# The perceptron of a two-layer decoder trunk takes x before its norm's row factor, and the planner that orders the kernel's instructions gets other costs

## The chip, the cores and the metric

One core of a Trainium2 chip runs the whole program. The metric is the device time of one execution in microseconds (us); lower is better. The shape is one sequence of 256 tokens, 1024 channels, two layers, float32.

## The reference, cut to what matters

Each layer has a mixing part (three branches whose merged result goes through `w_out`) and a perceptron with squared ReLU. Both are normed before and after:

```python
def rmsnorm(x, g):
    y = x * lax.rsqrt(jnp.mean(x * x, axis=-1, keepdims=True) + EPS)
    return y * g

for l in range(DEPTH):
    ...
    x = x + rmsnorm(merged @ w_out[l], ln_mix_post[l])
    h = rmsnorm(x, ln_mlp_pre[l])
    x = x + rmsnorm(jnp.square(jax.nn.relu(h @ mlp_w1[l])) @ mlp_w2[l], ln_mlp_post[l])
```

The norm multiplies each row of x by one positive number c (its row factor) and each column by a gain. As c is positive, relu(c·h) squared is c² times relu(h) squared, so c may be left out ahead of `mlp_w1` and c² be put on the result of `mlp_w2`.

## The kernel before

**Numbers and tiles.** Tokens are two tiles of 128 rows (t = 0, 1). Every float32 product runs as three products of parts: ScalarE copies an operand into a rounded part `hi`, VectorE subtracts it from the original into `lo`, and TensorE adds hi·hi, hi·lo and lo·hi in one PSUM bank. Weights come as units of 256 rows by 512 columns through SP's queue into five buffers (`raw`) and are split by ScalarE (`whi`) and VectorE (`wlo`) into four. Activations that stand as the contracted operand are needed transposed: four 128x128 transposes into a bank (`tr`), then the copy and the subtraction into `hmh` and `hml` (an object `XT`).

**The order of the work is planned while the program is built.** Side work is written as generators ("lanes") that yield the engine they want next ("A" ScalarE, "D" VectorE, "G" GpSimd, "P1" TensorE with one free bank). `Order` keeps a modelled clock for every engine, `Meter` (its call is line 140, so nearly all instructions of the trace carry that line) adds a modelled cost for each instruction, and after each weight row block (6 matmuls of 512 columns, or 12 of 256) `side` emits what the model says is ready by TensorE's modelled clock. `drain` forces a lane to its end where the next matmul needs it. Each engine then runs its instructions in the order in which they were emitted. The model's cost of a matmul of n columns is, in us,

```python
load = args[1].shape[1] / 1200.0
cost = max(load, 0.0025 + n / 2400.0) * (4 if args[1].dtype == F32 else 1)
```

and the modelled clock of the arrival of data is `dma_clock`.

**The jobs** follow each other in a written list per layer (`ORDER0`, `ORDER1`). Layer 0 starts `xr1 xr0 yr0 yr1 vm0 km0`: four projections of the normed x, then the keys and values of the memory tokens. The memory's norm is a lane that `mem_prep(0)` spawns during the first job, `start`, with a first due time of `dma_clock + 2.0`. It begins with a sum of squares of each loaded half tile of `mem` on ScalarE (`half_sumsq`, result tile `junk`); its transposes are needed at `vm0`.

**The boundary between mixing and perceptron.** `wo` multiplies by `w_out` into four banks, one for each token tile and half of the columns. When a bank is done, `Residual.half` sums its squares (ScalarE, `junk`) and multiplies it by the post-norm's gain (VectorE, `yg`). When both halves of a token tile are done, `finish` works out the row factor on GpSimd (`mean`, `var`, `rstd`) and adds the result to x (`xt`, VectorE). Then the next norm follows on the same engines in `norm_lane` and `half_lane`: sums of squares of the new x (`junk`), `mean`, `var`, `rstd`, the scaled row `hn` = x · factor · gain (VectorE), four transposes, two copies of 256 columns, two subtractions of 256 columns. `u0`, the first 512 columns of `mlp_w1`, needs them. In layer 0 the list puts `+vm0 +km0` (memory keys and values of layer 1) between `wo` and `u0`. In layer 1 nothing stands between, but there `wo` and `u0` run token tile 0 first and then token tile 1 (`skew`, `up_by_token`), so that one tile's boundary can run beside the other's matmuls; and `wo`'s weights can be split ahead of time into spare buffers (`we`). At the other boundary, after `d7`, the same `Residual` is used, followed by the next layer's norm, or in layer 1 by the store of the output.

Of the kernel before, what the change touches and what calls it, by code (L numbers as in the profile page):

```python
# [11 lines left out]
F32 = mybir.dt.float32  # L12
# [3 lines left out]
AF = mybir.ActivationFunctionType  # L16
# [89 lines left out]
class Meter:  # L106
# [5 lines left out]
    def __getattr__(self, name):  # L112
        fn, key, order = getattr(self.eng, name), self.key, self.order

        def call(*args, **kw):
            out = kw["out"] if "out" in kw else args[0]
            n = elems(out)
            if key == "A":
                cost = 0.055 + n / 1200.0
                cost += 0.06 * sum(not isinstance(kw.get(k, 0.0), float) for k in ("scale", "bias"))  # L120
                cost += 0.12 if kw.get("accum_out") is not None else 0.0
                if args[2] in TABLES:
                    cost += 1.28 * (self.table != TABLES[args[2]])
                    self.table = TABLES[args[2]]
            elif key == "D":
                if "reduce" in name:
                    n = elems(args[1])
                cost = DCOST + n / (1920.0 if name == "tensor_scalar" else 960.0)
                cost += 0.06 * (name == "scalar_tensor_tensor")
            elif key == "P":  # L130
                if name == "transpose":
                    cost = 0.109
                else:
                    load = args[1].shape[1] / 1200.0
                    cost = max(load, 0.0025 + n / 2400.0) * (4 if args[1].dtype == F32 else 1)
            else:
                cost = 0.25
            aps = [v.tensor.name for v in (*args, *kw.values()) if hasattr(v, "tensor")]
            order.note(key, cost, out.tensor.name, aps if "out" in kw else aps[1:])
            return fn(*args, **kw)  # L140

        return call
# [3 lines left out]
def trunk_kernel(ctx, tc, x, mem, positions, ln_mix_pre, w_in, conv_w, conv_b, lru_wr, lru_br, lru_wi, lru_bi,  # L146
# [48 lines left out]
    def f(ap):  # L195
        return ap.bitcast(F32)
# [191 lines left out]
            res.append(gt)  # L388
        return res

    def half_sumsq(src):

        j = a([P, 512], BF16, "junk")
        s = tiny([P, 1], name="ss")
        act.activation(j, src, AF.Square, scale=1.0 / 32, accum_out=s)
        return s

    def eps_lane(s, box):
        yield "G"
        m = tiny([P, 1], name="mean")  # L400
        pool.tensor_scalar(m, s, EPS, None, op0=OP.add)
        box.append(m)

    def first_half(src):

        box = []
        return spawn(eps_lane(half_sumsq(src), box), prio=0), box

    def rstd_of(m0, s1):
        v = tiny([P, 1], name="var")  # L410
# [108 lines left out]
    def normed(name):  # L519

        return lambda u, t: [f"{name}{v}{u // 2}" for v in range(NT) if t in (v, None)]

    class Residual:


        def __init__(self, t, tag, gt, g2, o, name):
            self.t, self.tag, self.gt, self.g2, self.o, self.name = t, tag, gt, g2, o, name
            self.g, self.ss = {}, {}

        def half(self, h, acc):  # L530
            def sums():
                yield "A"
                if h == 0:
                    el, self.box = first_half(acc)
                    yield el
                else:
                    self.s1 = half_sumsq(acc)

            def gain():
                yield "D"  # L540
                self.g[h] = a([P, 512], F32, "yg")
                dve.tensor_tensor(self.g[h], acc, self.gt[h], op=OP.mult)

            def both():
                yield [self.ss[h], gl]
                free(self.tag)

            self.ss[h] = spawn(sums(), prio=0)
            gl = spawn(gain(), prio=0)
            self.ss[h, "g"] = gl  # L550
            spawn(both(), prio=0)
            if h:
                spawn(self.finish(), prio=0)

        def finish(self):
            t = self.t
            yield [self.ss[0], self.ss[1]]
            yield "G"
            r = rstd_of(self.box[0], self.s1)
            ss = [None, None]  # L560

            def add(h):
                yield self.ss[h, "g"]
                yield "D"
                dve.scalar_tensor_tensor(xt[t][h], self.g[h], r, xt[t][h], op0=OP.mult, op1=OP.add)
                if self.o is None:
                    nc.sync.dma_start(out=out[0, t * P:(t + 1) * P, 512 * h:512 * h + 512], in_=xt[t][h])
                    return
                yield "A"
                if h == 0:  # L570
                    el, ss[0] = first_half(xt[t][0])
                    yield el
                else:
                    ss[1] = half_sumsq(xt[t][1])

            yield [spawn(add(h), prio=0) for h in range(2)]
            if self.o is not None:
                yield from norm_lane(xt[t], t, self.g2, self.o, self.name, ss)


# [763 lines left out]
    def layer(l):  # L1344
# [258 lines left out]
        def wo_done(t, hf, o):  # L1603
            if t == 0 and hf == 0:
                E["XM"] = XT("hm")
                E["res"] = [Residual(t, "at", *E["g_mix"], E["XM"], f"bnd{l}a") for t in range(NT)]
            E["res"][t].half(hf, o)
            if t == 1 and hf == 1:
                E["g_mlp_post"] = gain_tile(ln_mlp_post[l:l + 1, :])

        def wo_job():

            st = {}
            units = [Unit(w_out[l], 256 * k, 512 * hf) for k in range(4) for hf in range(2)]

            def begin():
                E["g_mix"] = gain_tile(ln_mix_post[l:l + 1, :]), gain_tile(ln_mlp_pre[l:l + 1, :])
                st["b"] = [[bank([P, 512], "at", "wo") for _ in range(2)] for _ in range(NT)]

            def mm(ui, u, i, only):  # L1620
                k, hf = 2 * (ui // 2) + i, ui % 2
                for t in range(NT) if only is None else (only,):
                    xh, xl = (v(k, t * P, (t + 1) * P) for v in (E["mg"].h, E["mg"].l))
                    o = st["b"][t][hf]
                    pe.matmul(o, xh, u.hi[i], start=(k == 0), stop=False)
                    pe.matmul(o, xh, u.lo[i], start=False, stop=False)
                    pe.matmul(o, xl, u.hi[i], start=False, stop=(k == KC - 1))
                    if k == KC - 1:
                        wo_done(t, hf, o)

            return Job(units, begin, mm, unit_need=lambda u, t: [f"mg{l}{u // 4}{v}" for v in range(NT) if t in (v, None)],
                       steps=[(u, t) for t in range(NT) for u in range(8)] if l == 1 else None, early=l == 1)
# [27 lines left out]
        def down_job(b):  # L1660
            units = [Unit(mlp_w2[l], 512 * b + 256 * kk, 512 * hf) for hf in range(2) for kk in range(2)]

            def begin():
                if b == 0:
                    E["acc"] = [[bank([P, 512], "at", "acc") for _ in range(2)] for _ in range(NT)]
                if b == 7:
                    g2 = o = None
                    if l + 1 < DEPTH:
                        g2, o = E["g_next"], XT("hT")
                        env[l + 1]["X"] = o  # L1670
                    E["res"] = [Residual(t, "at", E["g_mlp_post"], g2, o, f"bnd{l}b") for t in range(NT)]

            def mm(ui, u, i, only):
                hf, kk = ui // 2, ui % 2
# [66 lines left out]
        for b in range(8):  # L1741
            J[f"u{b}"], J[f"d{b}"] = up_job(b), down_job(b)

    def const_lane():
        yield "P1"
        pt = bank([P, P], "at", "pet")
        pe.transpose(pt, per.rearrange("p u d -> p (u d)"), ident)
        yield "D"
        dve.tensor_copy(pet, pt)
        free()  # L1750
        yield from rope_tables()

    def mem_prep(l):
        ms = []
        gm = gain_tile(ln_mem[l:l + 1, :])
        for t in range(NT):
            ms.append([])
            for h in range(2):
                m = a([P, 512], F32, "mem")
                nc.sync.dma_start(out=m, in_=mem[0, t * P:(t + 1) * P, 512 * h:512 * h + 512])  # L1760
                ms[t].append(m)
        env[l]["M"] = XT("mT")
        dma_clock[0] = max(dma_clock[0], od.T["D"] - 4.0) + 6 * 0.73
        od.cur.r = max(od.cur.r, dma_clock[0] + 2.0)
        spawn(norm_both(ms, gm, env[l]["M"], f"mnorm{l}"))

    def load_x(t):
# [28 lines left out]
    def start():  # L1796
        first_pre()
        mem_prep(0)
        prows = load_params()
        load_consts()  # L1800
        od.cur.r = 26.0
        spawn(prm_lane(prows), "prm")
        od.cur.r = 36.0
        spawn(const_lane(), "const")
# [35 lines left out]
```

## Time and profile before

| | us |
|---|---|
| median of 3 runs | 1221.04 |
| lowest and highest run | 1216.6, 1221.95 |
| the profiled execution's own time | 1221.59 |
| its span, first to last instruction | 1219.9 |

The mean granted TensorE clock over the span is 0.995 of full speed. PE is TensorE, ACT ScalarE, DVE VectorE, POOL GpSimd, SP the queue that issues DMAs. Matmuls are pipelined and their ends are modelled: a matmul that is listed with 283 ns can be followed by the next after 120 ns, so "busy" doesn't show small gaps.

### The profile page before, as it was taken

Reading aid. Unit: us, or ns where it says so; the run is one execution under the profiler, and the core shown is the slowest. Engines: PE = TensorE matmul, PEld = TensorE weight load, DVE = VectorE, ACT = ScalarE, POOL = GpSimd, SP = SyncE. Lnnn points to the kernel's source line nnn. Section 1 sums busy time; section 2 is a strip of 40 time slices with the busy share of each in tenths; the row PEclk is TensorE's granted clock in tenths of the full one; section 3 lists DMA queues with packets and bytes.
Section 4 is the critical chain, followed back from the end, with each engine's and each line's share of the span. In section 5 each row is a group of like instructions: output and inputs, shape, how many; then the busy total and the mean of one; then the engine's idle time right before and its main releaser. Section 6 shows DMA issues by size and latency. Waiting matters only on the chain.

```text
span 1219.9 us, 19570 instructions
## 1 busy us (share of the span) xinstructions
PE 1199.6 (98%) x7371; PEld 1068.8 (88%) x7371; DVE 901.6 (74%) x1516; ACT 736.7 (60%) x1330; POOL 35.5 (3%) x88
## 2 busy tenths in 40 slices
PE   8899999999999999999999999999999999999997
PEld 7899988888888889998989999888888887899896
DVE  4778897979898686555557587998978877655555
ACT  4677856777666465445456688675656655645443
POOL 3000000000000020000001000000000001000000
PEclk9899999999999999999999999999999999999999
DMA  8555656753345666666656556584534356565561
GB/s 283 181 161 168 190 156 181 223 152 108 122 131 186 233 191 191 194 189 189 206 174 210 154 171 176 153 258 140 154 121 138 121 164 217 166 187 183 190 190 69
DMA packets 121263, 212.58 MB, mean 174 GB/s; under 512 B 10441, under 2 KB 24098, under 8 KB 121169
## 3 DMA queue, kind: packets, MB, share of 16 engines
q1 hardware_dynamic: 120752, 211.19, 55.9%
q8 instruction: 58, 0.95, 0.3%
q0 software_dynamic: 416, 0.15, 0.1%
q14 instruction: 37, 0.30, 0.1%
HBM read 208.16 MB, written 1.05 MB: 172 GB/s over the span
## 4 chain that ended last, share of the span: by engine, by line
PE 92%; DVE 2%; DMA 2%; ACT 2%; issue 1%; SPq 0%; POOL 0%; POOLq 0%; DVEq 0%; ACTq 0%
PE mm L140 62%; PE acc L140 14%; PE ob L140 2%; PE sc L140 2%; PE wo L140 2%; PE pt L140 2%; PE hid L140 1%; PE gp L140 1%; PE mo L140 1%; PE msc L140 1%; PE tr L140 1%; DMA mem<-in_mem_dram 1%; ACT junk L140 1%; DVE wlo L140 1%; DMA raw<-in_mlp_w_dram 1%
## 5 line engine op out<-in xcount | busy, mean ns | idle before, releaser
L140 DVE TENSOR_TENSOR wlo<-raw,whi 128x1024 fp32r<-128x1024 f32 (+1 forms) x371 | 447.1, 1214 | 225.7 <-ACT whi L140 224.3
L140 ACT ACTIVATE whi<-raw 128x1024 fp32r<-128x1024 f32 (+1 forms) x371 | 385.3, 1055 | 204.9 <-PE mm L140 117.0
L140 PE MATMUL mm<-hmh,whi 128*128 128x256 f32 x480 | 135.9, 283 | 0.0
L140 PE MATMUL mm<-hmh,wlo 128*128 128x256 f32 x480 | 135.9, 283 | 0.0
L140 PE MATMUL mm<-hml,whi 128*128 128x256 f32 x480 | 135.9, 283 | 0.0
L140 PE MATMUL mm<-hTh,whi 128*128 128x256 f32 x448 | 129.4, 289 | 0.0
L140 PE MATMUL mm<-whi,hTh 128*128 128x512 f32 x320 | 129.1, 403 | 0.0
L140 PE MATMUL mm<-hTh,wlo 128*128 128x256 f32 x448 | 127.6, 285 | 0.0
L140 PE MATMUL mm<-hTl,whi 128*128 128x256 f32 x448 | 127.6, 285 | 0.0
L140 PE MATMUL mm<-wlo,hTh 128*128 128x512 f32 x320 | 125.1, 391 | 0.0
L140 PE MATMUL mm<-whi,hTl 128*128 128x512 f32 x320 | 125.0, 391 | 0.0
L140 PE MATMUL acc<-whi,rh 128*128 128x512 f32 x256 | 99.8, 390 | 0.0
L140 PE MATMUL acc<-wlo,rh 128*128 128x512 f32 x256 | 99.8, 390 | 0.0
L140 PE MATMUL acc<-whi,rl 128*128 128x512 f32 x256 | 99.6, 389 | 0.0
L140 PEld LDWEIGHTS mm<-hmh,whi 128*128 128x128 f32 x480 | 92.1, 192 | 0.5
L140 PEld LDWEIGHTS mm<-hml,whi 128*128 128x128 f32 x480 | 92.1, 192 | 0.5
L140 PEld LDWEIGHTS mm<-hmh,wlo 128*128 128x128 f32 x480 | 92.1, 192 | 0.0
L140 PEld LDWEIGHTS mm<-hTh,whi 128*128 128x128 f32 x448 | 86.9, 194 | 0.2
L140 PEld LDWEIGHTS mm<-hTl,whi 128*128 128x128 f32 x448 | 86.9, 194 | 0.2
L140 PEld LDWEIGHTS mm<-hTh,wlo 128*128 128x128 f32 x448 | 86.7, 194 | 0.0
L140 PEld LDWEIGHTS mm<-whi,hTl 128*128 128x128 f32 x320 | 60.1, 188 | 13.1
L140 PEld LDWEIGHTS mm<-whi,hTh 128*128 128x128 f32 x320 | 60.2, 188 | 12.0 <-issue 0.2
(311 smaller groups left out, 2467.7 us busy)
## 6 DMA issues: line engine op xcount, KB each, us to landing
raw<-in_w_in_dram SPq DMA_DIRECT2D x136, 512.0 KB, 3.7
raw<-in_mlp_w_dram SPq DMA_DIRECT2D x128, 512.0 KB, 4.2
raw<-in_w_mem_kv_dram SPq DMA_DIRECT2D x32, 512.0 KB, 4.2
raw<-in_cmp_w_dram SPq DMA_DIRECT2D x16, 512.0 KB, 4.0
raw<-in_w_br_rnn_dram SPq DMA_DIRECT2D x16, 512.0 KB, 3.7
raw<-in_w_br_mem_dram SPq DMA_DIRECT2D x16, 512.0 KB, 3.7
raw<-in_w_br_nsa_dram SPq DMA_DIRECT2D x16, 512.0 KB, 3.7
raw<-in_w_out_dram SPq DMA_DIRECT2D x16, 512.0 KB, 4.5
```

The source lines that it names most:

```text
L140: return fn(*args, **kw)
```

## The change

In five places:

1. `raw_lane` replaces `norm_lane` after `wo`: x itself is transposed, and the copy and the subtraction apply the pre-norm's gain as one number per partition (`col(k)`, from `mcol`, eight columns per layer). They are now made for 128 columns at a time, in turn: copy, subtraction, copy, subtraction, four pairs for each half. The row factor is made beside it in `factor_lane`, at lower priority.
2. The `Residual` behind `mlp_w2` takes that factor: its sums of squares read their scale from a tile, and the multiplication by the gain becomes one with the factor and the gain.
3. `mcol` needs one more small DMA on GpSimd's queue behind the ten that are there, one transpose and one copy at a planned 40 us. The broadcast gain tile of `ln_mlp_pre` (two DMAs of 256 KB per layer) goes.
4. The planner's cost of a matmul: 0.0133 in place of 0.0025 us beside the columns; for float32 operands 0.001.
5. The memory norm of layer 0 is due 12 us after `dma_clock` in place of 2 us. Layer 1 keeps 2 us.

```diff
-                    cost = max(load, 0.0025 + n / 2400.0) * (4 if args[1].dtype == F32 else 1)
+                    cost = (max(load, 0.0133 + n / 2400.0) if args[1].dtype != F32 else 4 * max(load, 0.001 + n / 2400.0))
...
+    def raw_lane(src, col, t, h, o):
+
+        yield "P1"
+        pt = bank([P, 4, P], "at", "tr")
+        for i in range(4):
+            pe.transpose(pt[:, i, :], src[:, i * P:(i + 1) * P], ident)
+        tq = slice(t * P, (t + 1) * P)
+        for i in range(4):
+            k = 4 * h + i
+            yield "A"
+            act.activation(o.h(k, t * P, (t + 1) * P), pt[:, i, :], AF.Copy, scale=col(k))
+            yield "D"
+            dve.scalar_tensor_tensor(o.l(k, t * P, (t + 1) * P), pt[:, i, :], col(k), f(o.h(k, t * P, (t + 1) * P)),
+                                     op0=OP.mult, op1=OP.subtract)
+        free()
+
+    def factor_lane(t, res):
+
+        yield "A"
+        el, box = first_half(xt[t][0])
+        s1 = half_sumsq(xt[t][1])
+        yield el
+        yield "G"
+        v = tiny([P, 1], name="var")
+        pool.tensor_tensor(v, box[0], s1, op=OP.add)
+        yield "D"
+        dve.reciprocal(res[:, 0:1], v)
+        dve.tensor_scalar(res[:, 1:2], res[:, 0:1], 1.0 / 32, None, op0=OP.mult)
...
-                dve.tensor_tensor(self.g[h], acc, self.gt[h], op=OP.mult)
+                if self.factor is None:
+                    dve.tensor_tensor(self.g[h], acc, self.gt[h], op=OP.mult)
+                else:
+                    dve.scalar_tensor_tensor(self.g[h], acc, self.factor[:, 0:1], self.gt[h], op0=OP.mult, op1=OP.mult)
...
+                if self.col is not None:
+                    yield spawn(raw_lane(xt[t][h], self.col, t, h, self.o), f"{self.name}{t}{h}", prio=0)
+                    return
...
-            if self.o is not None:
+            if self.col is not None:
+                yield spawn(factor_lane(t, self.res), f"{self.name}f{t}", prio=1)
+            elif self.o is not None:
                 yield from norm_lane(xt[t], t, self.g2, self.o, self.name, ss)
...
-                E["g_mix"] = gain_tile(ln_mix_post[l:l + 1, :]), gain_tile(ln_mlp_pre[l:l + 1, :])
+                E["g_mix"] = gain_tile(ln_mix_post[l:l + 1, :])
...
-                    E["res"] = [Residual(t, "at", E["g_mlp_post"], g2, o, f"bnd{l}b") for t in range(NT)]
+                    for t in range(NT):
+                        drain(f"bnd{l}af{t}")
+                    E["res"] = [Residual(t, "at", E["g_mlp_post"], g2, o, f"bnd{l}b", factor=E["r2"][t]) for t in range(NT)]
...
-        od.cur.r = max(od.cur.r, dma_clock[0] + 2.0)
+        od.cur.r = max(od.cur.r, dma_clock[0] + (2.0 if l else 12.0))
...
+        row = a([8 * DEPTH, P], F32, "mrow")
+        nc.gpsimd.dma_start(out=row, in_=ln_mlp_pre.rearrange("l (k c) -> (l k) c", c=P))
+        od.cur.r = 40.0
+        spawn(mcol_lane(row), "mcol")
```

## Rows read from the trace of the kernel before

**Rows 1.** Page: busy us, share of the span and instructions of each engine.
```profile
PE 1199.6 (98%) x7371; PEld 1068.8 (88%) x7371; DVE 901.6 (74%) x1516; ACT 736.7 (60%) x1330; POOL 35.5 (3%) x88
```

**Rows 2.** Windows by stage: length, busy us of five engines, PE clock, DMA share, GB/s.
```profile
0.00:50.00 50.00, 41.02 (x291) 40.27 (x292) 27.65 (x64) 27.14 (x52) 13.22 (x40) 0.90 0.74 238
...
210.00:410.00 200.00, 199.91 (x1101) 168.31 (x1100) 171.72 (x345) 136.47 (x316) 1.89 (x6) 1.00 0.51 158
410.00:446.00 36.00, 36.00 (x171) 29.97 (x170) 25.46 (x32) 19.01 (x35) 7.27 (x12) 1.00 0.66 217
...
780.00:1006.00 226.00, 224.61 (x1228) 188.53 (x1227) 196.08 (x392) 141.08 (x314) 0.00 (x0) 1.00 0.51 155
...
1026.00:1040.00 14.00, 11.20 (x57) 8.65 (x56) 7.70 (x15) 7.56 (x23) 3.49 (x9) 1.00 0.18 62
```

**Rows 3.** Waits of PE: what waited for what, us in total, times, longest.
```profile
PE tr L140 <- DVE hn L140: 9.2, 5, 3.2
...
PE gn L140 <- DVE wlo L140: 0.9, 1, 0.9
```

**Rows 4.** Timeline of ACT, 0 to 56 us: start, us, instructions, [idle before, releaser].
```profile
20.11 1.06 ACT L140 ACTIVATE whi<-raw 128x1024 fp32r<-128x1024 f32 x1 [0.74 <-PE mm L140]
28.34 0.63 ACT L140 ACTIVATE junk<-mem 128x512 bf16<-128x512 f32 x1 [7.17 <-DMA mem<-in_mem_dram]
...
31.95 2.00 ACT L140 ACTIVATE whi<-raw 128x1024 fp32r<-128x1024 f32 x2
```

**Rows 5.** Windows around the first stall of PE, columns as in Rows 2.
```profile
34.97:40.78 5.81, 5.81 (x27) 5.81 (x28) 5.60 (x14) 2.36 (x6) 0.00 (x0) 0.50 0.91 266
31.65:42.17 10.52, 7.36 (x42) 7.20 (x41) 8.72 (x23) 4.81 (x10) 0.42 (x1) 0.68 0.59 168
```

**Rows 6.** Instructions on tile raw, 22.7 to 22.8 us: the next weight unit behind mem.
```profile
L341 SPq DMA_DIRECT2D raw<-in_w_in_dram x1: 613/613/613, 22.8 to 22.8; - x1
DMA to landing us min/median/max: 8.9/8.9/8.9
```

**Rows 7.** Chain that ended last, whole span, in order of time: start, us, what.
```profile
42.42 8.63 PE mm L140 x72
...
250.48 1.59 PE mm L140 x6
254.88 1.38 PE mm L140 x6
...
1079.60 10.91 PE acc L140 x48
```

**Rows 8.** The same chain at layer 1's boundary, 1000 to 1062 us.
```profile
1024.72 0.76 DVE xt L140
...
1027.90 0.76 DVE hn L140
...
1028.71 0.67 PE tr L140 x4
...
1029.40 0.67 ACT hmh L140 x2
...
1030.09 0.04 DVE hml L140
...
1031.51 0.64 DVE yg L140
...
1032.17 0.70 ACT junk L140 x2
```

**Rows 9.** ACT's groups with shapes kept apart: busy us, mean ns, idle before.
```profile
L140 ACT ACTIVATE hTh<-tr,gcol 128x256 fp32r<-128x256 f32 x8 | 3.2, 479 | 2.7 <-PE tr L140 2.7
...
L140 ACT ACTIVATE hid<-hidT 128x128 f32<-128x128 f32 x6 | 1.4, 276 | 4.9 <-PE hidT L140 4.9
```

**Rows 10.** DVE's groups with shapes kept apart, columns as in Rows 9.
```profile
L140 DVE SCALAR_TENSOR_TENSOR hTl<-tr,gcol,hTh 128x256 fp32r<-128x256 f32 x8 | 3.3, 476 | 1.3 <-ACT hTh L140 1.3
...
L140 DVE TENSOR_TENSOR vx<-mm,vx 128x128 fp32r<-128x128 f32 x16 | 3.8, 278 | 0.0
```

More of the change, by code (lines that the diff above doesn't have):

```diff
@@ L389, in gain_tile, with half_sumsq @@
         return res
-    def half_sumsq(src):
+    def half_sumsq(src, scale=1.0 / 32):
         j = a([P, 512], BF16, "junk")
         s = tiny([P, 1], name="ss")
-        act.activation(j, src, AF.Square, scale=1.0 / 32, accum_out=s)
+        act.activation(j, src, AF.Square, scale=scale, accum_out=s)
         return s
@@ L402, in eps_lane, with first_half @@
         box.append(m)
-    def first_half(src):
+    def first_half(src, scale=1.0 / 32):
         box = []
-        return spawn(eps_lane(half_sumsq(src), box), prio=0), box
+        return spawn(eps_lane(half_sumsq(src, scale), box), prio=0), box
     def rstd_of(m0, s1):
@@ L521, in normed, with __init__ @@
         return lambda u, t: [f"{name}{v}{u // 2}" for v in range(NT) if t in (v, None)]
+    def raw_lane(src, col, t, h, o):
[23 more added lines that the diff above has]
+        dve.tensor_scalar(res[:, 1:2], res[:, 0:1], 1.0 / 32, None, op0=OP.mult)
     class Residual:
-        def __init__(self, t, tag, gt, g2, o, name):
+        def __init__(self, t, tag, gt, g2, o, name, factor=None, col=None, res=None):
             self.t, self.tag, self.gt, self.g2, self.o, self.name = t, tag, gt, g2, o, name
+            self.factor, self.col, self.res = factor, col, res
+            self.scale = 1.0 / 32 if factor is None else factor[:, 1:2]
             self.g, self.ss = {}, {}
@@ L533, in sums @@
                 if h == 0:
-                    el, self.box = first_half(acc)
+                    el, self.box = first_half(acc, self.scale)
                     yield el
                 else:
-                    self.s1 = half_sumsq(acc)
+                    self.s1 = half_sumsq(acc, self.scale)
             def gain():
@@ L1605, in wo_done @@
                 E["XM"] = XT("hm")
-                E["res"] = [Residual(t, "at", *E["g_mix"], E["XM"], f"bnd{l}a") for t in range(NT)]
+                E["r2"] = [sp.tile([P, 2], F32, tag="r2", bufs=2 * NT, name=nm("r2")) for _ in range(NT)]
+                col = lambda k: mcol[:, 8 * l + k:8 * l + k + 1]
+                E["res"] = [Residual(t, "at", E["g_mix"], None, E["XM"], f"bnd{l}a", col=col, res=E["r2"][t])
+                            for t in range(NT)]
             E["res"][t].half(hf, o)
@@ L1742, in layer, with mcol_lane @@
             J[f"u{b}"], J[f"d{b}"] = up_job(b), down_job(b)
+    mcol = cp.tile([P, 8 * DEPTH], F32, name="mcol")
+    def mcol_lane(row):
+        yield "P1"
+        pt = bank([P, 8 * DEPTH], "at", "mcol")
+        pe.transpose(pt, row, ident[:8 * DEPTH, :8 * DEPTH])
+        yield "D"
+        dve.tensor_copy(mcol, pt)
+        free()
     def const_lane():
```

## The prediction

> **What bounds the kernel now.** I read the page first. TensorE is busy for 1199.6 of 1219.9 us, VectorE 74%, ScalarE 60% [rows 1]: time can only come from where PE waits, or runs slowly. [...] So I counted waits and rates, in this order.
>
> The windows by stage show where PE is not busy: 9.0 us of the first 50, 0.1 of the 200 us from 210, nothing at layer 0's boundary (410 to 446), 1.4 from 780 to 1006, 2.8 of the 14 us at layer 1's boundary (1026 to 1040) [rows 2]. The list of PE's waits puts 9.2 us, five waits, on transposes `tr` that wait for `hn`, the scaled rows of a norm; the longest is 3.2 us. Next comes one wait of 0.9 us for `wlo` [rows 3]. Two places hold nearly all that the change can win.
>
> The first is at 31.7 us. ScalarE ends a weight copy at 21.2 us, and the next thing in its queue is the first sum of squares of `mem`, whose data land at 28.3: 7.2 us idle. The weight unit that PE needs next is copied only at 31.95, behind the four sums [rows 4]. [...] The second is layer 1's boundary: in the chain `xt` (1024.72) is followed by sums, factor and `hn` (1027.90), and only then by `tr` (1028.71) [rows 8].
>
> **The change part by part. The memory norm due 10 us later.** ScalarE was free for its sums at 21.2, so their due time lay no later than about there; 10 us on is 31.2 us or more, and the data land at 28.3 [rows 4], 2.9 us before. The weight copies then go first. Their data: the unit queued behind `mem` was issued at 22.75 and landed 8.9 us later [rows 6], at 31.7. A copy takes 1.0 us (2.00 for two [rows 4]), and I take the subtraction of the same width a little longer, at 1.2, so the unit stands at about 34, while PE, with the units split before it, needs it at 31.7 + 24 · 0.120 = 34.5 (0.120 us is 8.63/72 [rows 7]). A thin margin, but one.
>
> What is won: between 31.65 and 42.17 PE did 24 matmuls of 256 columns and 16 transposes (the count of 42 has two that began before) [rows 5]. At the full rate the matmuls are 2.9 us, and the transposes, of 128 columns, at no more than the same 0.120, 1.9: together 4.8. They took 10.5: 5.7 us to win, of which some 3.2 are the wait and the rest clock. What is late next is the transposes again, 10 us later in PE's order. ScalarE now reaches the sums only behind two weight copies that can't begin before 31.7, at about 34, and the chain from sums to transposes is 3.2 us (from the end of `xt`'s first half, 1024.72 + 0.76, to 1028.71 [rows 8]): 37.2. In the plan the sums stood between the weight copy that ended at 21.2 and the result of the first job some 4 us later, so their new place is 31.2 to 35, the middle 33.2, and by the model's own costs (two sums of 0.6, two GpSimd steps of 0.25, 0.66 for `hn`, the changes of engine) the transposes follow 3.0 to 3.2 later, at 36.4. PE would wait about 0.8 us; side work enters only after 12 matmuls, a grid of 1.4 us, so 0 to 2.2. I take 5.7 − 0.8 = **4.9 us won**, bounds 3.5 and 5.7.
>
> **x without the row factor, layer 0.** PE has no idle time at that boundary, since `vm0 km0` (two times some 11 us of matmuls) cover it [rows 2]. Nothing to win. If the cover were gone the new path would cost what it does in layer 1.
>
> **The same in layer 1.** Removed from the path: two sums, `mean`, `var`, `rstd` and `hn`. `tr` can follow the first half of `xt`, 1024.72 + 0.76 = 1025.5, and not wait until 1028.7: 3.2 us earlier [rows 8]. Added: the four pairs of copy and subtraction. Today two copies of 256 columns run from 1029.40 to 1030.07, and only then, 0.02 us later, does the first subtraction start, though its own copy was done a third of a microsecond before; and at 1032.17 a sum of squares starts just as the product of the same bank ends [rows 8]. So ScalarE and VectorE take turns on a bank. [...]
>
> Prices: no copy of 128 columns with a column of scales stands in the trace; it lies between 0.276 (128 columns, no such operand) and 0.479 us (256 with it) [rows 9], and I take 0.36, nearer the smaller. The subtraction lies between 0.278 and 0.476 [rows 10]; I take 0.34. With two handovers of 0.03 a pair takes 0.76, four 3.0 us, and with 0.67 for the transposes a half is ready 3.7 us after `tr` starts; today about 2.1 (1028.71 to some 1030.8). So 1.6 of the 3.2 us go back, bounds 0.9 and 2.6. PE's idle 2.8 us arise twice, once for each token tile. For tile 0 the transposes no longer hold up `wo`'s last matmuls, and its split is late by at most a microsecond. For tile 1 `xt` comes 2.4 us after `wo`'s last product (1031.51 to 1033.9 now), the half 0.7 + 3.7 us later, and 24 matmuls of 0.227 (10.91/48 [rows 7]) with 8 transposes, 6.3 us, cover most of these 6.8. `factor_lane`'s sums may slip in between. I take **2.4 us won**, bounds 0.5 and 3.3.
>
> **`mlp_w2`'s side.** The product by the gain stays one pass; the sums get a scale from a tile, some 0.1 us once in the tail after the last matmul, where nothing hides it: **0.1 lost**. In layer 0 matmuls hide it. The factor is made a whole perceptron before it is needed. `mcol` is one transpose (0.11 us of PE, in the rounding). Its DMA stands last in GpSimd's queue; nothing is behind it. The gain tile's two DMAs leave SP's queue in front of the perceptron's first weights: no loss, perhaps a gain in the term above.
>
> **The planner's costs.** By the rows a matmul of 512 columns takes 0.227 and of 256 0.120 us; the model had 0.216 and 0.109, the new one gives 0.227 and 0.120. Side work on PE is now put in 5 to 10% earlier counted in matmuls. A side chain of 2 us thus loses 0.1 to 0.2 us of reserve it had by accident. But work enters on the grid of 1.4 us, so only some 10% of about 150 groups between 210 and 1006 (by the code's loops 48 of scores, 48 of transposed probabilities, 32 of products, and smaller ones) move to an earlier slot, where a wait of 0.1 us or so may arise: about 1.5 us at most. Against this stand waits that may go (0.9 us [rows 3], pieces with 0.2 us hidden [rows 7]). I take **0**, bounds 3 won and 4 lost.
>
> **Sum.** 1221.6 (the profiled execution's own time) − 4.9 − 2.4 + 0.1 + 0 = 1214.4. That execution stood 0.55 above the median of the runs, so 1213.9.
>
> **The rivals.** 0.5% is 6.1 us, about what a measurement of this kernel can tell from no change; faster begins at 1214.9.
>
> 1. *The start's gain goes back.* If the transposes come more than 2 us after their place, or the late weight unit (margin 0.5 us) holds PE, PE waits as long as before and the clock falls again. For it: the same wait of 3.2 us was followed by the 0.50 clock [rows 3, 5]. Against it: the data land 2.9 us ahead of the sums' place. Start 0 to 1 won: 1221.0 − 0.5 − 2.3 = about 1218.5.
> 2. *The boundary gives nothing*, since eight turns on one bank with sums and splits between take the 3.2 us back. It decides if a pair takes 1.1 us and not 0.76. 1221.0 − 4.9 + 0.5 = about 1216.6.
> 3. *The truer order also takes waits away*: 0.9 us at `gn`, some ten pieces with 0.2 us: 2 to 4 us more, 1210 to 1212.
> 4. *Slower: the accidental reserve was needed.* If each of some 150 groups of side work between 210 and 1006 comes 0.1 us too early, PE waits 15 us in pieces of 0.1, and 1214 becomes 1229. It decides from 13 us of such waits. Against it: these 426 us hold only 1.5 us of idle PE now [rows 2], so most chains have room.
>
> **How the numbers follow.** Both gains as summed 0.55 (own range 1211 to 1217), rival 1 0.18, rival 2 0.13, rival 3 0.09, rival 4 0.05. The likeliest gives 1213.9. Leaving out rival 4, the slow end of rival 1 and the fast end of rival 3 gives 1210 to 1219.5. Faster than 1214.9: eight tenths of the likeliest, since its sum lies a microsecond below, and rival 3: 0.53. Slower: rival 4 and a trace of rival 1: 0.07. The same: 0.40.
>
> **What would show it.** Right: ScalarE's sums of `mem` after 31 us with no wait for the DMA, PE without a gap over 2 us and at clock 1.00 from 30 to 42 us, `vm0` some 5 us earlier; in layer 1 `tr` straight behind `xt`, PE's waits for it under 0.5 us, `u0` ended some 7 us earlier than now. Wrong: PE waiting for `tr` or for a weight unit near 35 us; `hml` the last thing before `u0`; many new waits of PE of 0.1 to 0.3 us on scores and transposes between 210 and 1006. The sum also fails if the runs before the change are fast by luck of their clock, as the lowest of the three (1216.6) may be.

## The result and the profile after

The change made the kernel slower: 1234.22 us median (1231.84 to 1234.47, 6 runs) against 1219.29 (1215.06 to 1221.95, 6 runs), ratio 1.0121, interval 1.0097 to 1.0145. The forecast was 1213.9 us with a range up to 1219.5, and slower had 0.07 of the chance. The profiled execution of after took 1234.42 us, its span is 1232.7: 12.8 more than before's.

The same rows as [rows 1] and [rows 2], of after. First the page's line of TensorE, then the windows by stage, with the same columns.

```profile
PE 1206.5 (98%) x7372; PEld 1069.8 (87%) x7372; DVE 905.5 (73%) x1547; ACT 736.6 (60%) x1332; POOL 34.1 (3%) x85
```
```profile
0.00:50.00 50.00, 44.69 (x335) 43.81 (x336) 34.50 (x90) 29.59 (x54) 15.54 (x41) 1.00 0.79 257
210.00:410.00 200.00, 196.62 (x1078) 163.58 (x1077) 172.48 (x355) 128.97 (x302) 1.89 (x6) 1.00 0.49 152
410.00:446.00 36.00, 36.00 (x172) 29.94 (x171) 24.15 (x31) 16.08 (x27) 2.97 (x6) 1.00 0.66 213
780.00:1006.00 226.00, 223.31 (x1213) 186.48 (x1212) 194.36 (x398) 144.56 (x317) 0.00 (x0) 1.00 0.49 151
1026.00:1040.00 14.00, 12.51 (x58) 10.05 (x56) 11.66 (x16) 8.22 (x14) 1.44 (x3) 1.00 0.91 309
```

The start stands where the forecast put it: 335 matmuls in the first 50 us and not 291, at clock 1.00 (how much of that the change won is asked below). But from 210 to 410 us, where PE had been idle for 0.1 us, it is now idle for 3.4 and does 1078 matmuls in place of 1101. The waits of PE answer to [rows 3].

```profile
PE mm L140 <- DVE wlo L140: 8.6, 10, 3.2
PE tr L140 <- DVE hn L140: 3.1, 3, 2.1
...
PE tr L140 <- DVE xt L140: 1.5, 1, 1.5
PE pt L140 <- DVE pl L140: 1.3, 1, 1.3
PE hid L140 <- DVE wlo L140: 0.8, 1, 0.8
```

`hn` fell from 9.2 to 3.1 us. In its place stands `mm` waiting for `wlo`, the low part of a weight split: 8.6 us, ten times, up to 3.2 us. Every kernel here does the same 5952 matmuls on the tiles `mm`, `acc`, `wo` and `gn`, so I compared starts at equal counts of them. Minus is ahead of the kernel before; the names behind *after* are those of experiments below.

```
matmuls  before at     after  cost_alone  all_but_cost  all_scaled
    288      56.7       -5.2       -3.1          -4.1        -1.7
    480      88.3       -4.2       -2.1          -3.1        -1.5
    864     147.4       +1.4       +1.9          -2.7        -3.1
   1632     378.2       +4.4       +5.2          -2.5        -2.5
   2016     460.8       +5.3       +7.1          -2.4        -2.5
   3168     640.1       +5.3       +7.1          -2.4        -2.5
   4128     804.2      +13.2      +15.1          -2.3        +2.0
   4704     992.9      +14.4      +16.2          -2.0        +2.2
   4896    1045.1      +12.8      +19.3          -0.1        +1.5
   5856    1191.5      +12.8      +19.3          -0.1        +1.5
```

The loss arises in the two mixers, between 90 and 410 us and between 640 and 810; in the perceptrons, which have few side chains, the distance stays constant to 0.1 us. From the first row to 993 us cost_alone loses as much as after, 19.3 us against 19.6; it ends later since it stands 2.1 us less ahead at the start and loses another 3.1 at layer 1's boundary, where after wins 1.6.

**One stall read whole.** At 138 us PE waits for a split. The timelines of ScalarE, VectorE and PE, and one window with the columns of [rows 2], all of after:

```profile
132.02 1.06 ACT L140 ACTIVATE whi<-raw 128x1024 fp32r<-128x1024 f32 x1
```
```profile
133.62 1.22 DVE L140 TENSOR_TENSOR wlo<-raw,whi 128x1024 fp32r<-128x1024 f32 x1
134.79 0.33 DVE L140 TENSOR_TENSOR gs<-g,pet 128x120 f32<-128x120 f32 x1
...
135.04 0.90 DVE L140 TENSOR_TENSOR gs<-g,pet 128x120 f32<-128x120 f32 x3
135.85 0.69 DVE L140 TENSOR_TENSOR oal<-gelu,oah 128x512 fp32r<-128x512 f32 x1
136.45 0.69 DVE L140 SCALAR_TENSOR_TENSOR ti<-th,ti 128x512 f32<-128x512 f32 x1
137.18 1.27 DVE L140 TENSOR_TENSOR_SCAN xc<-aa,ti 128x256 f32<-128x256 f32 x2
138.49 0.69 DVE L140 SCALAR_TENSOR_TENSOR gelu<-xc,gelu 128x512 f32<-128x512 f32 x1
139.09 2.35 DVE L140 TENSOR_TENSOR wlo<-raw,whi 128x1024 fp32r<-128x1024 f32 x2
```
```profile
138.15 0.39 PE L140 MATMUL mm<-whi,mTh 128*128 128x512 f32 x1
140.37 0.50 PE L140 MATMUL mm<-wlo,mTh 128*128 128x512 f32 x1 [1.83 <-DVE wlo L140]
```
```profile
140.70:144.10 3.40, 3.40 (x10) 2.69 (x9) 3.40 (x6) 2.13 (x5) 0.00 (x0) 0.56 0.76 228
```

Read it backwards. PE needs `wlo` at 138.5 (138.15 + 0.39) and gets it at 140.3, when the first of the two subtractions listed at 139.09 ends. A unit's copy and subtraction are emitted together, so the n-th `whi` and the n-th `wlo` of a run belong together; the input of this `wlo` is the copy of 132.02, done at 133.08. VectorE ends the subtraction before it at 134.8 and then goes, without a gap, through 4.3 us of side work (`gs`, `oal`, `ti`, `xc`, `gelu`) before it begins this one at 139.09, 6.0 us after its input was ready. Directly behind the subtraction before, it would have been done at about 136.1, in time. Here VectorE keeps to the emitted order: `wlo`, ready for 6.0 us, passes none of that work. Behind the stall the granted clock is 0.56 on average over 3.4 us, with 10 matmuls where 0.227 us each would give 15.

The same unit in before, on ScalarE, VectorE and PE:

```profile
138.66 1.06 ACT L140 ACTIVATE whi<-raw 128x1024 fp32r<-128x1024 f32 x1
```
```profile
140.37 1.21 DVE L140 TENSOR_TENSOR wlo<-raw,whi 128x1024 fp32r<-128x1024 f32 x1
```
```profile
142.17 0.39 PE L140 MATMUL mm<-wlo,mTh 128*128 128x512 f32 x1
```

There the subtraction begins 0.65 us after its copy's end and is done 0.6 us before PE takes it, without a wait.

### The profile page after: what moved, and what is told of

Same layout as the page of the kernel before. It is cut to its first block, busy times and chain, and to the rows that moved or that the text cites. A ratio compares the mean times of both kernels' runs of the same rounds, so it can differ in the third digit from the quotient of the medians.

```text
span 1232.7 us, 19612 instructions
## 1 busy us (share of the span) xinstructions
PE 1206.5 (98%) x7372; PEld 1069.8 (87%) x7372; DVE 905.5 (73%) x1547; ACT 736.6 (60%) x1332; POOL 34.1 (3%) x85
## 4 chain that ended last, share of the span: by engine, by line
PE 85%; DVE 6%; ACT 5%; issue 2%; DMA 1%; SPq 1%; POOL 0%; DVEq 0%; POOLq 0%; ACTq 0%
PE mm L140 56%; PE acc L140 14%; PE wo L140 2%; PE sc L140 2%; PE ob L140 2%; DVE wlo L140 2%; PE pt L140 2%; ACT whi L140 1%; PE mo L140 1%; PE tr L140 1%; PE gp L140 1%; PE hid L140 1%; PE msc L140 1%; DVE rt L140 1%; PE csc L140 1%
## 5 line engine op out<-in xcount | busy, mean ns | idle before, releaser
L140 ACT ACTIVATE pr<-sc,mx 128x256 f32<-128x256 f32 (+1 forms) x128 | 52.1, 428 | 38.6 <-DVE mx L140 38.6
L140 PEld LDWEIGHTS mm<-wlo,hTh 128*128 128x128 f32 x320 | 60.2, 188 | 14.7 <-DVE wlo L140 4.7
```

## The experiments

Each was compared with the kernel before on the same chip (medians 1217.5 to 1218.5 us there). Theory 1: the dearer matmul lets the plan's PE clock run ahead, so more side work enters the order ahead of the weight splits. Rivals: the two other parts; one false duration (the shuffle of the compressed keys, booked at 3 us, whose transfers take 8 us in after, from the first issue at 126.6 us to the last landing at 134.6); a lucky order before.

**The parts apart.**

```diff
cost_alone:   before, with
-  cost = max(load, 0.0025 + n / 2400.0) * (4 if args[1].dtype == F32 else 1)
+  cost = (max(load, 0.0133 + n / 2400.0) if args[1].dtype != F32 else 4 * max(load, 0.001 + n / 2400.0))
all_but_cost: after, with that line turned back
due_alone:    before, with
-  od.cur.r = max(od.cur.r, dma_clock[0] + 2.0)
+  od.cur.r = max(od.cur.r, dma_clock[0] + (2.0 if l else 12.0))
raw_alone:    after, with both lines turned back (raw x only)
```

> The kernel before with nothing but the new cost of a matmul in the planner. Theory 1 (the cost formula puts side work earlier on VectorE and ScalarE, so the weight splits come late and PE waits for wlo): all of the loss and none of the two gains, 1232 to 1242 us, PE waiting for wlo in several places between 110 and 1006 us. Theory 2 (the shifted start makes later work collide): 1217 to 1222 us, no such waits. Theory 3 (the perceptron's edit disturbs the order): 1217 to 1222 us.

> The changed kernel with the old cost of a matmul in the planner: the later memory norm and x without the row factor alone. Theory 1: both gains and no loss, 1210 to 1215 us. Theories 2 and 3: as slow as the whole change, 1230 to 1236 us.

> The kernel before with nothing but the memory norm of layer 0 due 10 us later. Theory 1: the start's gain alone, 1213 to 1216 us, no idle PE of over 2 us between 30 and 42 us. Theory 2: the gain is there at 60 us and gone again by 240 us, 1220 to 1232 us. Theory 3: 1213 to 1216 us.

> The kernel before with nothing but x taken without the row factor (and its factor, mcol and gain edits). Theories 1 and 2: only layer 1's boundary changes, 1.5 to 3 us won, 1216 to 1218 us. Theory 3: 1225 to 1235 us.

Measured: cost_alone 1241.19 us, ratio 1.0192 (interval 1.0176 to 1.0208); all_but_cost 1220.08, 1.0016 (1.0006 to 1.0025); due_alone 1218.74, 1.0007 (0.9997 to 1.0018); raw_alone 1219.08, 1.0004 (0.9993 to 1.0016). The cost is the whole loss. In cost_alone the waits for `wlo` are those of after; the waits for `hn`, which fell in after, are as large as in before:

```profile
PE tr L140 <- DVE hn L140: 9.1, 7, 2.8
PE mm L140 <- DVE wlo L140: 8.5, 8, 3.6
```

The three other expectations missed: both forecast gains measure as nothing. For the start, look at raw_alone, whose start isn't touched. Timelines of ScalarE and PE, and the window of [rows 5]:

```profile
27.34 0.63 ACT L140 ACTIVATE junk<-mem 128x512 bf16<-128x512 f32 x1 [5.64 <-DMA mem<-in_mem_dram]
```
```profile
33.83 0.66 PE L140 MATMUL tr<-ident,hn 128*128 128x128 f32 x4 [1.49 <-DVE hn L140]
```
```profile
34.97:40.78 5.81, 5.81 (x52) 5.81 (x52) 5.50 (x16) 4.43 (x11) 0.00 (x0) 1.00 0.82 256
```

Here `mem` landed a microsecond sooner than in [rows 4], PE waited 1.49 us and not 3.16, and its clock stayed at 1.00: 52 matmuls in the window that holds 27 in [rows 5]. The execution from which the start was costed was an unlucky one. In all twelve experiments with the norm due at its old place `mem` came between 25.19 and 27.63 us, in none as late as 28.34. That execution took 1221.6 us; the median of 25 runs is 1218.5. And raw_alone's profile, with the old start, stands 3.4 us ahead of it at its 56.7 us; due_alone's stands 4.3 ahead.

At layer 1's boundary all_but_cost lost what it should have won (ScalarE, PE and VectorE in order of time, then a window):

```profile
1020.36 1.07 ACT L140 ACTIVATE whi<-raw 128x1024 fp32r<-128x1024 f32 x1 [1.58 <-DMA raw<-in_mlp_w_dram]
1021.33 0.58 ACT L140 ACTIVATE junk<-wo 128x512 bf16<-128x512 f32 x1
...
1024.59 0.66 PE L140 MATMUL tr<-ident,xt 128*128 128x128 f32 x4 [2.88 <-DVE xt L140]
...
1025.29 0.37 ACT L140 ACTIVATE hmh<-tr,mcol 128x128 fp32r<-128x128 f32 x1 [2.71 <-PE tr L140]
...
1025.69 0.35 DVE L140 SCALAR_TENSOR_TENSOR hml<-tr,mcol,hmh 128x128 fp32r<-128x128 f32 x1 [0.49 <-ACT hmh L140]
...
1026.08 0.37 ACT L140 ACTIVATE hmh<-tr,mcol 128x128 fp32r<-128x128 f32 x1 [0.42 <-DVE hml L140]
```
```profile
1024.59:1028.00 3.41, 3.41 (x14) 2.92 (x15) 1.93 (x5) 1.71 (x6) 0.00 (x0) 0.64 0.77 289
```

The sums stand behind a weight copy that waits for its data, `xt` is late, and the transposes of it stand in PE's queue ahead of `wo` matmuls that were ready. PE waits 2.88 us, then runs at a mean clock of 0.64. The pair of copy and subtraction takes 0.79 us (1025.29 to 1026.08) against the 0.76 forecast.

```diff
boundary_later: all_but_cost, with, in Residual.finish
             r = rstd_of(self.box[0], self.s1)
+            od.cur.r += 2.0 if self.col is not None else 0.0
```

> The changed kernel with the old matmul cost, and the residual sum of the perceptron's input booked 2 us later, so that the transposes of x stand behind some nine matmuls of the output projection that were ready while TensorE waited 2.9 us for x at layer 1's boundary, and its clock fell for 3.4 us. If the boundary's gain was lost to that wait and to the clock: 1213 to 1217 us, without either. Rival (the wait goes to the first hidden unit, since the transposes end later): 1219 to 1222 us, as without the edit (1220).

Measured 1218.26 us, ratio 1.0002 (0.999 to 1.0015). PE waits less and keeps its clock:

```profile
1024.44 1.32 PE L140 MATMUL tr<-ident,xt 128*128 128x128 f32 x8 [1.19 <-DVE xt L140]
```
```profile
1024.59:1028.00 3.41, 3.40 (x19) 2.73 (x19) 2.15 (x7) 2.13 (x7) 0.00 (x0) 1.00 0.80 274
```

1.8 us came back by the medians, less than expected and more than the rival allowed, though the intervals of the two ratios overlap: a wait of 1.19 us stayed. In the profiles the boundary turns from 1.9 us lost into 1.1 won. With it the changed parts are as fast as the kernel before, not faster. No version beat it.

**Which relation of the costs.**

```diff
shuffle_8:    cost_alone, with   od.cur.r += 8.0   for 3.0 behind the shuffle's transfers
queue_half:   cost_alone, with   HORIZON = 1.5     for 3.0
wide_only:    before, with
+  cost = max(load, (0.0133 if n == 512 and args[1].dtype != F32 else 0.0025) + n / 2400.0) * (4 if args[1].dtype == F32 else 1)
all_scaled:   cost_alone, nearly every other duration, rate, due time and limit of the plan x 1.065
ad_scaled:    cost_alone, with
+  cost *= 1.065 if key in "AD" else 1.0
rest_scaled:  all_scaled without that line's operations
side_dearer:  before, old matmul cost, with ad_scaled's line
side_cheaper: before, old matmul cost, with 0.939 in it
after_scaled: after, scaled as all_scaled
```

> The kernel before with the new matmul cost, and the shuffle of the compressed keys booked at 8 us in place of 3 us. Rival, shuffle (the one false duration that bites is the shuffle's; the dearer matmul only moved it to where it blocks VectorE): the stalls at about 138 and 760 us go, with their clock drops and the late order behind them: 1220 to 1228 us. Theory 1 (all side work is let in too early): those two stalls go, 4 to 8 us, the rest stays: 1232 to 1238 us.

> The kernel before with the new matmul cost, and ScalarE, VectorE and GpSimd booked at most 1.5 us ahead of TensorE in place of 3 us. Theory 1 in its narrow form (side work booked up to 3 us ahead stands in front of the weight splits in the two in-order queues): half the booking gives half the delay, waits for weight splits fall from 8.5 us to under 4 us: 1222 to 1234 us. Rivals (shuffle, lucky order): no gain, 1236 to 1246 us, since less booking ahead also delays side work that TensorE needs.

> The kernel before with the new cost for matmuls of 512 columns only (5% more); those of 256 columns keep the old cost (10% less than the new). Theory 1 (each percent of the ratio counts, wherever it is): the time lies between, 1224 to 1236 us, and the stalls in stretches of 256-column matmuls (138, 220 to 240, 760 to 790 us) are smaller than with the whole cost. Rival, lucky order: 1230 to 1242 us, with stalls in other places.

> The kernel before with the new matmul cost, and every other duration of the plan (ScalarE, VectorE, GpSimd, transposes, the waits between engines, the DMA rate, due times, the 3 us by which an engine may be booked ahead) longer by 6.5%, which is between what a 512-column matmul (5%) and a 256-column one (10%) gain. Theory 1 (what hurts is the ratio of the matmul's cost to the other costs, which were all too low together: side work is let into the order too early per matmul): 1216 to 1226 us, near the kernel before, with under 4 us of TensorE's waits for weight splits. Rival, lucky order (the order of before is one good draw, and any other order of the same work costs 1 to 2%): 1230 to 1242 us, as the new cost alone (1241).

Measured: shuffle_8 1239.13 us, 1.0164 (1.0138 to 1.0189); queue_half 1246.2, 1.0223 (1.0196 to 1.0249); wide_only 1225.47, 1.0052 (1.0032 to 1.0072); all_scaled 1222.23, 1.0031 (1.002 to 1.0041). The shuffle is worth 2 us, not clear of nothing (the interval overlaps cost_alone's): its rival falls, and so do the 4 to 8 us I gave it. In shuffle_8 the waits of `mm` for `wlo` do fall, from 8.5 to 5.0 us and the longest from 3.6 to 1.1, with little gain in time. In queue_half they fall as expected, to 1.3 us, but waits for side chains take their place (`pt` for `pl` alone 4.8 us) and nothing is won, so the narrow form of theory 1 falls too. wide_only ends in the range of theory 1 and below its rival's. all_scaled takes 19 of the 23 us back. That is near to a change of unit, which would leave the order alone; what it shows is that the absolute size of the matmul's cost does little harm. Its first waits of PE:

```profile
PE tr L140 <- DVE hn L140: 8.1, 6, 2.8
PE warm L140 <- DVE dmask L140: 2.5, 1, 2.5
PE hid L140 <- ACT whi L140: 1.6, 1, 1.6
```

> The changed kernel whole (later memory norm, raw x, new matmul cost), with every other duration of the plan longer by 6.5% as well. Theory 1 (the ratio of the costs is what made the change slow): 1215 to 1225 us, as the changed kernel with the old cost (1220). Rival (the new cost hurts the new parts in its own way, by where their steps fall): 1228 to 1236 us, as the changed kernel (1234).

> The kernel before with the new matmul cost, and only the operations of ScalarE and VectorE longer by 6.5%; GpSimd, transposes, the waits between engines, the DMA rate, due times and the booking ahead stay. Theory 1 (the lists of the two busy side engines against TensorE's matmuls are what counts): 1218 to 1228 us. Rival (the waits between engines or the DMA terms are what counts): 1233 to 1242 us.

> The kernel before, with the old matmul cost, and the operations of ScalarE and VectorE longer by 6.5%. Theory 1 with a direction (too much side work per matmul is let in when the matmul is dear against it; the other way does no harm, side work has slack): 1214 to 1224 us. Theory 1 without a direction, or lucky order: 1228 to 1240 us.

> The kernel before, with the old matmul cost, and the operations of ScalarE and VectorE shorter by 6.1%, so that the ratio to the matmul is that of the kernel with the new cost alone. Theory 1: 1230 to 1242 us, with waits for weight splits and clock drops as with the new cost alone (1241), though the matmul's cost isn't touched. Rival (a dearer matmul hurts through what it alone sets, TensorE's own clock against the DMA's): 1216 to 1226 us.

> The kernel before with the new matmul cost, and everything but the operations of ScalarE and VectorE longer by 6.5% (GpSimd, transposes, waits between engines, DMA rate, due times, booking ahead): the complement of the run that raised those two alone and lost as much. Balance of all the durations at once: 1230 to 1242 us. Rival (only the waits, transposes and DMA terms must move with the matmul): 1217 to 1226 us.

Measured: after_scaled 1221.07 us, 1.0028 (1.0017 to 1.0039); ad_scaled 1243.0, 1.0214 (1.0197 to 1.023); side_dearer 1244.92, 1.0231 (1.0208 to 1.0254); side_cheaper 1238.78, 1.0175 (1.0154 to 1.0195); rest_scaled 1245.63, 1.0228 (1.0207 to 1.0249). side_cheaper and after_scaled fit theory 1; ad_scaled, and in side_dearer the direction that I gave it, don't; rest_scaled lost even more than its range (1230 to 1242). Dearer side work loses at least as much as cheaper, and giving ScalarE and VectorE alone, or all but them, the matmul's rise helps nothing. With side work dear, PE waits more for what side chains deliver than for weights: in side_dearer 14.1 us against 3.8, `hn` and the start's `dmask` apart; in cost_alone 2.7 against 10.1. Some of its waits in side_dearer:

```profile
PE tr L140 <- DVE hn L140: 5.1, 4, 3.3
PE mm L140 <- DVE vx L140: 3.6, 1, 3.6
...
PE mm L140 <- DVE obl L140: 2.3, 3, 1.1
PE ob L140 <- ACT ct L140: 1.7, 3, 0.7
...
PE mm L140 <- DVE wlo L140: 0.7, 2, 0.5
```

**Dose.** Left was whether any reordering loses (a lucky order) or whether the loss grows with the distance (a balance).

```diff
fifth, half: before, with 0.0047 and 0.0079 for 0.0025 (cost_alone has 0.0133);
             float32 operands keep the old cost (cost_alone has 0.001 for them)
```

> The kernel before with a fifth of the matmul's rise (0.0047 us for 0.0025; 1% at 512 columns, 2% at 256). Balance (the loss grows with the distance from the old relation of the costs): 1218 to 1224 us. Lucky order (any reordering loses what the others lost): 1230 to 1244 us.

> The kernel before with half of the matmul's rise (0.0079 us for 0.0025). Balance: 1225 to 1234 us, between the kernel before (1218) and the whole rise (1241). Lucky order: 1230 to 1244 us, no nearer to before than the whole rise is.

Measured: fifth 1222.45 us, 1.0037 (1.0025 to 1.0049); half 1233.94, 1.0133 (1.0116 to 1.0149). The loss grows with the dose. So the lucky order falls in the form in which any reordering loses what the others lost: fifth lies far below the 1230 to 1244 us expected of it (half lies in the ranges of both). For each of the 387 subtractions `wlo` and `we` I summed the durations of VectorE's other work ordered ahead of it, and took the difference to the kernel before. I also counted the subtractions between which and the one before them VectorE has other side work than in the kernel before.

```
                     fifth   half  cost_alone  after
median over before    +4.7  +16.2       +22.7  +14.9   us
side work ahead, mean +1.3   +3.1        +5.7   +4.8   us
mm waits for wlo       0.9    2.6         8.5    8.6   us
other side work        156    171         186    185   of 387
```

Displacement alone doesn't tell the time. wide_only has a mean of +5.8 us and loses only 0.5%; due_alone and raw_alone have +1.5 and +1.3, as fifth has, and lose nothing; queue_half and side_dearer have 0.0 and −0.4 and lose 2.2 and 2.3%. The count of changed places follows the times better: 30 to 62 in the four versions with the old costs (within 0.2% of before), 119 to 156 in all_scaled, after_scaled, wide_only and fifth (0.3 to 0.5% lost), 171 to 192 in the nine others, after among them (1.2 to 2.3%). So a milder lucky order, one tuned around the old costs of which each reordering loses a share, fits the times as well as a balance of the costs does. No run here separates the two, or the places where the displacement falls.

## Why the prediction was wrong

- **The planner's costs, taken as 0 with at most 4 lost, is the step that failed.** It alone loses 22.7 us, and some 13 on top of the other parts (ratio 1.0121 against 1.0016). The step reckoned that a side chain loses 0.1 to 0.2 us of reserve and that some 10% of 150 groups move by one slot. But far more moved: in after VectorE's side work is another at 185 of 387 splits (60 in all_but_cost), and on average 4.8 us more of it stands ahead of a split (1.3). That bookings add up, since by the code an engine's booked time is carried from group to group, would explain it; no run shows that by itself. I counted side work that PE waits for; what became late in after was the weight split, which shares the queues of ScalarE and VectorE with that side work and, in the stall at 139.09, stood ready for 6.0 us behind it: PE's waits for parts of weights, each over 0.15 us, sum to 10.3 us there and to 3.3 in all_but_cost.
- **Rival 4** had the sign, with 0.05, but another mechanism: 150 waits of 0.1 us. Between 210 and 410 us the gaps of 0.03 to 0.15 us in PE's starts sum to about 8.0 us in after, 7.7 before. Over the whole span all waits of PE over 0.15 us sum to 19.7 us in after and 12.3 in all_but_cost, 7.4 of the 13.0 us between these two profiles, most of it in a few waits of 0.3 to 3.2 us; the clock is slow at two of them (0.56 on average from 140.70 to 144.10 us, 0.50 from 763 to 764), and the rest is in starts that come late by less.
- **Rival 3** and the word "truer" misled: the matmul's new cost is right by the rows (0.227 and 0.120 us), and its relations to the other costs became worse for this order. The time follows the order, not how near one estimate is.
- **The start, 4.9 us.** After stands 5.2 us ahead at 56.7 us, and the steps are as told: sums at 32.09 behind the copies, PE busy all of the 29 us from 28 to 57. The size was taken from one unlucky execution, so that the profile agrees with it is luck; in the median due_alone wins nothing (its interval is 0.4 us faster to 2.2 slower). Its profiled execution is 4.3 us ahead at 57 us, 2.5 at 100, 1.4 at the end; that of raw_alone, with the old start, 3.4 at 57 and 3.4 at 100.

```profile
29.82 1.06 ACT L140 ACTIVATE whi<-raw 128x1024 fp32r<-128x1024 f32 x1 [0.79 <-DMA raw<-in_w_in_dram]
31.12 1.06 ACT L140 ACTIVATE whi<-raw 128x1024 fp32r<-128x1024 f32 x1 [0.25 <-DMA raw<-in_w_in_dram]
32.09 0.61 ACT L140 ACTIVATE junk<-mem 128x512 bf16<-128x512 f32 x1
...
34.54 1.04 ACT L140 ACTIVATE whi<-raw 128x1024 fp32r<-128x1024 f32 x1
```

- **Layer 1's boundary, 2.4 us.** Won were 1.6 in after (+14.4 to +12.8 in the table), 1.1 in raw_alone; in all_but_cost 1.9 were lost. The pair's price held. Overlooked was that the transposes now wait for `xt` itself, with ready matmuls behind them. VectorE and PE at that place in after:

```profile
1036.44 1.23 DVE L140 TENSOR_TENSOR wlo<-raw,whi 128x1024 fp32r<-128x1024 f32 x1 [0.63 <-ACT whi L140]
1037.59 1.28 DVE L140 TENSOR_TENSOR yg<-wo,gain 128x512 f32<-128x512 f32 x2
1038.79 1.41 DVE L140 SCALAR_TENSOR_TENSOR xt<-yg,rstd,xt 128x512 f32<-128x512 f32 x2
```
```profile
1037.70 0.39 PE L140 MATMUL wo<-we,mgl 128*128 128x512 f32 x1
1039.58 1.32 PE L140 MATMUL tr<-ident,xt 128*128 128x128 f32 x8 [1.49 <-DVE xt L140]
```

- **Layer 0's boundary and the tail** (nothing, and 0.1 lost) held: PE has no idle time from 410 to 446 us, the distance is +5.3 on both sides of the boundary, and the distance stays +12.8 to the end; a sum of squares of the tail, with its scale from a tile, takes 0.688 us in after and 0.597 in before.

**Open.** Why the best point known is the old relation, with the matmul 5 to 10% too cheap: a job order and due times chosen around the old plan would explain it, and no other order was tried. Nor was the float32 half of the cost line run alone; fifth and half leave it out and lose already.

## What to carry to other kernels

Where a cost model writes the order, a cost is a setting and not only a measurement: correct all that enter the same comparison together, or one at a small dose, and expect a change of 10% in one to move whole queues. Before costing a stall from a profile, look whether other executions have it at that size; a wait for a transfer and the clock behind it can be a bad draw (3.16 us and 0.50 in before's profile, 1.49 us and 1.00 in raw_alone's). To judge an earlier or later step, ask what stands behind it in its engine's queue, the feed of the main engine above all: here a weight split, ready for 6.0 us (after), and `wo` matmuls, while PE waited 2.88 us (all_but_cost).

## Unexpected of the hardware

- The same load of `mem` (first issue at 17.72 us in before) was first used between 25.19 and 28.34 us in thirteen profiles with the norm due at its old place; PE's first wait behind it was 3.16 us with the clock at 0.50 after it in one (before), and 1.49 us with the clock at 1.00 in another (raw_alone).
- The granted clock was 0.50 behind waits of 3.16 us (before at 34.97, until 40.78) and 3.22 (after at 762.59, from 763 to 764), 0.56 on average from 140.70 to 144.10 behind 1.83 (after at 140.37) and 0.64 on average from 1024.59 to 1028.00 behind 2.88 (all_but_cost). It was 1.00 behind two of 1.49 (raw_alone at 33.83, until 42.17; after at 1039.58, until 1045). But it was also 1.00 behind one of 2.15 us (after at 9.98, until 16): the length of the wait alone doesn't tell.
